# A hybrid attention block on one core: order of the last operand splits and division of the final normalisation

## The chip, the cores and the metric

The kernel runs on one core of one Trainium2 chip. The metric is the device time of one execution in microseconds (us), the median over the runs of a comparison. A profile of one execution is read beside it: every instruction of TensorE (PE), VectorE (DVE), ScalarE (ACT), GpSimd (POOL) and of the DMA queues, with start and duration.

## The reference

One encoder layer on 1024 tokens of width 1024. The input is projected once; the columns are queries, keys, values and gates of two groups of heads. Group A attends over a neighbourhood on a 16 x 64 grid, group B over a window of 128 tokens with a sink. Each output is multiplied by SiLU of its gate, then projected, added to the scaled input and normalised:

```python
h = jnp.einsum('bsd,de->bse', x, w_in[layer])
...
mixed = jnp.concatenate([y_a * jax.nn.silu(z_a), y_b * jax.nn.silu(z_b)], axis=-1)
y = jnp.einsum('bse,ed->bsd', mixed, w_out[layer])
x = layer_norm(DEEPNORM_ALPHA * x + y, ln_gain[layer], ln_bias[layer])
```

layer_norm takes mean and variance over the 1024 columns of a token, and ends with gain and bias.

## The kernel before, in words

**Arithmetic.** Products on PE are made of halves: a float32 operand is split into a float16 high part, `h`, and a low part, `l`, which is the float32 value less `h`. A product is three matmuls, high by high, high by low and low by high. For a split ACT casts the high part and DVE or POOL subtracts.

**Stages.** Input projection, attention over 128 units with the rest of the projection filled in between the units (`pump_to`, L1076), and the output projection with the normalisation (`final`, L1325). Each engine runs its instructions in the order in which the program gives them; ahead of `final` that order comes from a planner with costs and due times (`Op`, `enq`, `pop`), in `final` it is written out by hand (L1440 to L1540).

**Output projection.** It is a seven-product scheme on halves of tokens and of columns. The mixed activations lie transposed in eight z tiles, 128 inner columns by 1024 tokens, taken as four pairs (za, zb) (`ZP`, L43). `ZL` is tokens 0 to 511, `ZH` 512 to 1023. Of each pair come A11 (za, ZL), A12 (zb, ZL), A22 (zb, ZH), S3 = za ZL - za ZH, S2 = zb ZH - S3, S1 = za ZH + zb ZH and S4 = zb ZL - S2; S3, S2, S1 and S4 are made in place, in za ZL, za ZL, za ZH and zb ZL. The weights give B11, B21, B22 and T1 to T4. The products (`TERMS`, L1293) are q1 = A11 B11, q2 = A12 B21, q3 = S4 B22, p4 = A22 T4, q5 = S1 T1, q6 = S2 T2 and q7 = S3 T3, each summed over the four pairs. A product for one tile of 128 tokens is 12 matmuls of 512 columns. `prod` (L1298) issues them; its matmuls are all L1308.

**Banks.** Products share PSUM banks: b[t] takes q1, then q6, then q7, then p4; cb[t] takes q5, then q3; a[t] takes q2. Between two of them `add` (L1341) reads the bank on DVE and adds it, scaled, to the 512 columns of an output row tile in SBUF (`xr`, which holds alpha times the input): `add(t, a, ...)` for row tile t and column half a. So the next product in a bank waits for that addition. q1 of all tiles, and all but the last pair of q2 for tiles 0 and 1, are under way when `final` begins.

**Last pair.** z tiles 2 and 3 are done last. `m_last` (L1542) makes what is still to be made of them, with `za` for tile 2 and `z` for tile 3. `hi` is a cast on ACT (L1549), `lo` a subtraction on DVE or POOL (L1552). `first` scales row tile 0 by alpha on ACT; `between` is the first addition, `add(0, 0, b[0])`, which reads q1. Ahead of it in `final` DVE fills `eps` and `nident`, the negative identity (L1328 to L1331). PE then goes on with q5 for the first three pairs, q2's last pair for tiles 0 and 1 (L1493, L1494), q6(0), q5's last pair, q7(0), q3(0), q6(1) and so on. Loads of the row tiles 5, 2, 6, 3 and 7 (`x_load`, L1334) stand on SP's queue, in that order, with gain and bias between.

**Normalisation.** As a half row gets its last addition (`whole=True`), `bn` takes statistics of it in chunks. `row_stats` and `row_scale` give mean and reciprocal deviation. `norm` (L1415) splits the work of a row tile between DVE (columns 512 to 1023, with gain and bias copied into PSUM as gp and bp) and ACT with POOL (columns 0 to 511; tiles 0, 4 and 7 all columns). Row tile 7 and then row tile 3 are last. For tile 7 ACT normalises two halves (L1423), and POOL multiplies by the gain and adds the bias (`norm_half`, L1432). For tile 3 the last 512 columns of the product come in three parts of 256, 128 and 128: `norm_last` (L1377) does columns 512 to 1023 and 384 to 511 on DVE with PSUM copies of gain and bias (gp, bp, gq), and columns 0 to 383 on PE, as a sum of three products with the identity: row times gain (the gain multiplied in ahead by POOL, `norm_ahead`, L1374), minus mean times gain, plus deviation times bias; ACT scales it out. Matmuls on a zero tile `warm` keep PE running before that (L1380). Four output transfers end the kernel: tile 3 in three parts (L1401, L1403, and L1404 on ACT's queue) and tile 7's second half (L1438).

Of the kernel before, what the change touches and what calls it, by code (L numbers as in the profile page):

```python
# [7 lines left out]
F32 = mybir.dt.float32  # L8
# [4 lines left out]
AF = mybir.ActivationFunctionType  # L13
# [9 lines left out]
EPS = 1e-5  # L23
# [47 lines left out]
def hybrid_block(ctx, tc, xT, x, wt, wv, wo, bias, sink, gain, lbias, cos, sin, bmask, out):  # L71
    nc = tc.nc
# [37 lines left out]

    identf = const.tile([128, 128], F32, name="identf")
    make_identity(nc, identf)
    vb = zp.tile([128, 8, 2, 2, HD], F16, tag="zv", name="vb", bufs=1)
    vsc = const.tile([128, 1], F32, name="vsc")
    vrs = const.tile([128, 1], F32, name="vrs")
# [23 lines left out]
    nc.vector.memset(warm, 0.0)  # L139
    ones = const.tile([128, 128], BF16, name="ones")  # L140
    nc.vector.memset(ones, 2.0 ** -13)
    bm = const.tile([128, 320], F32, name="bm")
    sk = const.tile([128, 4], F32, name="sk")
    nsk = const.tile([128, 4], F32, name="nsk")
# [1180 lines left out]
    def final():  # L1325
        actx.close()
        fp = ctx.enter_context(tc.tile_pool(name="fp", bufs=2, reuse_waits="tile"))
        eps = fp.tile([128, 1], F32, name="eps", bufs=1)  # L1328
        nc.vector.memset(eps, EPS)
        nident = fp.tile([128, 128], F32, name="nident", bufs=1)  # L1330
        nc.vector.tensor_scalar_mul(nident, identf, -1.0)  # L1331
        xrs, stats = xr_, {}

        def x_load(t):  # L1334
# [14 lines left out]
        def bn(t, a, c):  # L1349
            o, w = c  # L1350
            if t not in stats:
                stats[t] = fp.tile([128, 8, 6], F32, name=f"stats{t}", bufs=1)
            b = 128 if t == 3 else 512
            for i in range(w // b):
                n = (512 * a + o) // b + i
                nc.vector.bn_stats(stats[t][:, n, :], xrs[t][:, b * n:b * n + b])

        def row_stats(t):
            mv = fp.tile([128, 2], F32, tag="mv", name="mv")
            nc.vector.bn_aggr(mv, stats[t][:, :8 if t == 3 else 2, :])  # L1360
            sd = fp.tile([128, 1], F32, tag="sd", name="sd")
            nc.scalar.activation(sd, mv[:, 1:2], AF.Sqrt, bias=eps)
            return mv, sd
# [5 lines left out]
            nc.vector.tensor_scalar(nmr, mv[:, 0:1], rstd, -1.0, op0=ALU.mult, op1=ALU.mult)  # L1369
            return rstd, nmr  # L1370

        HP, HQ, H1 = slice(0, 384), slice(384, 512), slice(512, 1024)

        def norm_ahead(t):  # L1374
            nc.gpsimd.tensor_mul(xrs[t][:, HP], xrs[t][:, HP], gb[:, HP])
# [1 line left out]
        def norm_last(t):  # L1377
            ts = slice(128 * t, 128 * t + 128)
            xr, pn = xrs[t], bank("t")
            for _ in range(28):  # L1380
                nc.tensor.matmul(gq[:, :128], warm, warm, start=True, stop=True)
            nc.tensor.matmul(pn[:, HP], identf, xr[:, HP], start=True, stop=False)
            dm, ds = (fp.tile([128, 128], F32, name=n, bufs=1) for n in ("dm", "ds"))
            mv = fp.tile([128, 2], F32, tag="mv", name="mv")
            nc.vector.bn_aggr(mv, stats[t])
            sd = fp.tile([128, 1], F32, tag="sd", name="sd")
            nc.scalar.activation(dm, nident, AF.Copy, scale=mv[:, 0:1])
            nc.scalar.activation(sd, mv[:, 1:2], AF.Sqrt, bias=eps)
            nc.scalar.activation(ds, identf, AF.Copy, scale=sd)
            rstd = fp.tile([128, 1], F32, tag="rstd", name="rstd")  # L1390
            nc.tensor.matmul(pn[:, HP], dm, gb[:, HP], start=False, stop=False)
            nc.tensor.matmul(pn[:, HP], ds, bb[:, HP], start=False, stop=True)
            halves = (H1, gp, bp), (HQ, gq[:, 128:256], gq[:, 256:384])
            for h, g, _ in halves:
                nc.vector.scalar_tensor_tensor(xr[:, h], xr[:, h], mv[:, 0:1], g, op0=ALU.subtract, op1=ALU.mult)
                if h is H1:
                    nc.vector.reciprocal(rstd, sd)
            for h, _, o in halves:
                nc.vector.scalar_tensor_tensor(xr[:, h], xr[:, h], rstd, o, op0=ALU.mult, op1=ALU.add)
                if h is H1:  # L1400
                    nc.sync.dma_start(out[ts, h], xr[:, h])  # L1401
            nc.scalar.activation(xr[:, HP], pn[:, HP], AF.Copy, scale=rstd)
            nc.sync.dma_start(out[ts, HQ], xr[:, HQ])  # L1403
            nc.scalar.dma_start(out[ts, HP], xr[:, HP])  # L1404
# [10 lines left out]
        def norm(t, *st_):  # L1415
            ts = slice(128 * t, 128 * t + 128)
            xr, ha, hb = xrs[t], slice(512, 1024), slice(0, 512)
            mv, sd = st_ or row_stats(t)
            rstd, nmr = row_scale(mv, sd)
            both = t in (0, 4, 7)  # L1420
            h = slice(0, 1024) if both else hb
            for h in (hb, ha) if t == 7 else (h,):
                nc.scalar.activation(xr[:, h], xr[:, h], AF.Identity, bias=nmr, scale=rstd)  # L1423
            if not both:
                nc.vector.scalar_tensor_tensor(xr[:, ha], xr[:, ha], mv[:, 0:1], gp, op0=ALU.subtract, op1=ALU.mult)
                nc.vector.scalar_tensor_tensor(xr[:, ha], xr[:, ha], rstd, bp, op0=ALU.mult, op1=ALU.add)
                nc.sync.dma_start(out[ts, ha], xr[:, ha])
            for h in (ha, hb) if both else (hb,):
                if t != 7:
                    norm_half(t, h)  # L1430

        def norm_half(t, h, between=None):  # L1432
            xr = xrs[t]
            nc.gpsimd.tensor_mul(xr[:, h], xr[:, h], gb[:, h])  # L1434
            if between:
                between()
            nc.gpsimd.tensor_add(xr[:, h], xr[:, h], bb[:, h])
            nc.sync.dma_start(out[128 * t:128 * t + 128, h], xr[:, h])  # L1438
# [82 lines left out]
        q7(2)  # L1521
        c11(2)
        gq = bank("s")
        nc.scalar.copy(gq[:, 128:256], gb[:, HQ])
        nc.scalar.copy(gq[:, 256:384], bb[:, HQ])
        q3(2)
        q6(3)
        p4(2)
# [13 lines left out]
    def m_last(first, between):  # L1542
        z, za = zt[ZP[3][1]], zt[ZP[3][0]]
        need(*done["S3", 3])
        for key in ("A12", "A22", "S1", "S2", "S4"):
            m_home(key, 3)

        def hi(key, src):
            nc.scalar.copy(part[key, 3][0], src)  # L1549

        def lo(eng, key, src):
            eng.tensor_sub(part[key, 3][1], src, part[key, 3][0])  # L1552

        hi("A12", z[:, ZL])
        first()
        nc.vector.tensor_sub(za[:, ZL], z[:, ZH], za[:, ZL])  # L1556
        nc.gpsimd.tensor_add(za[:, ZH], za[:, ZH], z[:, ZH])
        lo(nc.vector, "A12", z[:, ZL])
        hi("S2", za[:, ZL])
        hi("A22", z[:, ZH])  # L1560
        nc.vector.tensor_sub(z[:, ZL], z[:, ZL], za[:, ZL])
        between()
        lo(nc.vector, "S2", za[:, ZL])
        lo(nc.gpsimd, "A22", z[:, ZH])
        hi("S4", z[:, ZL])
        lo(nc.vector, "S4", z[:, ZL])
        hi("S1", za[:, ZH])
        lo(nc.gpsimd, "S1", za[:, ZH])

    fill.extend((out_head((0,), range(3), "pj"), out_head((1,), range(3), "pj"), out_head((0, 1), (3,), None),  # L1570
                 out_head((0,), range(3), "s", "q2"), out_head((1,), range(3), "s", "q2"),
# [190 lines left out]
```

## Time and profile before

| what | us |
|---|---|
| runs | 435.64, 436.56, 436.87 |
| median | 436.56 |
| the profiled execution | 434.77 |
| its span | 432.9 |
| PE busy | 425.5 |
| DVE busy | 347.6 |
| ACT busy | 315.9 |
| POOL busy | 291.2 |

In lines of the timeline the first number is the start in us from the span's start, the second the time to the end of the group; then engine, line of the kernel, operation, and output <- inputs by tile name with shapes; x is the count of instructions merged. Square brackets hold the idle time of the engine before the group, and what ended it. In lines of a group the numbers are durations in ns (least, median, greatest) and the first and last start. In lines of a window come its bounds and length, the busy time and count of PE, weight loads, DVE, ACT and POOL, then PE's granted clock, the busy share of the 16 DMA engines and GB/s.

### The profile page before, as it was taken

To read this page: it belongs to the slowest core of one execution; us is meant where nothing else is said; L and a number is where in the kernel's file an instruction comes from. 1 tells how busy PE (TensorE), PEld (TensorE's weight loads), DVE (VectorE), ACT (ScalarE), POOL (GpSimd) and SP (SyncE) were. 2 spreads that over 40 slices of the span, in tenths; PEclk is the share of its full clock that TensorE was granted. 3 is DMA by queue.
4 is the path that set the end of the run, shared out by engine and by line. 5 is a ranking of instruction groups with operands and counts; after the bars stand their busy time and mean duration, and the time that the engine had idled before them with its cause. 6 is when DMAs were issued, how large, how long until landed. Compare 5 with 4: busy or idle time off the path is not lost.

```text
span 432.9 us, 9414 instructions
## 1 busy us (share of the span) xinstructions
PE 425.5 (98%) x3197; PEld 249.3 (58%) x3197; DVE 347.6 (80%) x861; ACT 315.9 (73%) x677; POOL 291.2 (67%) x298
## 2 busy tenths in 40 slices
PE   9999999999999999999999999999999999899995
PEld 8997754444455656565556555565655655344444
DVE  5978976884987879888788997878888876787685
ACT  5849779787669989788988868889788883643222
POOL 0110085778568767879999976767889799458245
PEclk9999999999999999999999999999999999999999
DMA  7947759982349999989879999997999899923122
GB/s 267 406 145 256 238 177 324 286 269 89 118 140 190 205 157 209 210 186 151 171 167 221 199 196 176 249 182 141 221 186 214 149 143 281 414 111 123 73 98 99
DMA packets 131409, 84.82 MB, mean 196 GB/s; under 512 B 97568, under 2 KB 106656, under 8 KB 131360
## 3 DMA queue, kind: packets, MB, share of 16 engines
q1 hardware_dynamic: 131216, 84.02, 79.8%
q8 instruction: 25, 0.41, 0.4%
q14 instruction: 24, 0.20, 0.2%
q10 hardware_dynamic: 144, 0.20, 0.1%
HBM read 50.60 MB, written 10.52 MB: 141 GB/s over the span
## 4 chain that ended last, share of the span: by engine, by line
PE 95%; DVE 2%; POOL 1%; issue 0%; POOLq 0%; ACT 0%; ACTq 0%
PE ps_pj L457 50%; PE ps_t L996 7%; PE ps_s L1308 6%; PE ps_s L564 6%; PE ps_pj L1308 5%; PE ps_s L919 4%; PE ps_s L920 4%; PE ps_t L1308 3%; PE ps_pj L564 3%; PE ps_t L564 3%; PE ps_t L1033 2%; PE ps_t L490 1%; POOL xr L1434 1%; DVE A L1552 0%; DVE z L1556 0%
## 5 line engine op out<-in xcount | busy, mean ns | idle before, releaser
L457 PE MATMUL ps_pj<-xf,wh 128*128 128x512 f16 x672 | 201.3, 379 | 0.0
L457 PE MATMUL ps_pj<-xf,wl 128*128 128x512 f16 x336 | 127.3, 379 | 0.0
L457 PEld LDWEIGHTS <-wh 128*128 128x128 f16 x672 | 63.8, 98 | 58.3
L949 ACT ACTIVATE ps_s<-sn,nm 128x321 f32<-128x321 f32 (+3 forms) x128 | 67.7, 529 | 33.5 <-DVE nm L933 32.3
L968 DVE SCALAR_TENSOR_TENSOR split<-ps_s,split 128x320 f16<-128x320 f32 (+2 forms) x128 | 62.6, 489 | 17.9 <-ACT split L967 16.2
L253 POOL TENSOR_SCALAR wr<-wr,wsc 128x512 f32<-128x512 f32 x32 | 24.0, 749 | 56.3 <-ACT wh L248 48.5
L967 ACT ACTIVATE split<-ps_s 128x320 f16<-128x320 f32 (+2 forms) x128 | 55.1, 430 | 2.0 <-DMA tr<-split 0.4
L457 PEld LDWEIGHTS <-wl 128*128 128x128 f16 x336 | 32.9, 98 | 37.8
L933 DVE CUSTOM_DVE_ANT_0 sn<-ps_s,bm,nsk 128x320 f32<-128x320 f32 (+2 forms) x64 | 36.9, 577 | 9.9 <-PE ps_s L920 9.7
L254 POOL TENSOR_TENSOR wl<-wr,wh 128x512 f16<-128x512 f32 x32 | 39.6, 1238 | 2.7
L933 DVE CUSTOM_DVE_ANT_0 sn<-ps_s,bias,sg 128x368 f32<-128x368 f32 (+1 forms) x64 | 36.1, 564 | 4.4 <-PE ps_s L920 4.0
L920 PE MATMUL ps_s<-ks,qs 128*128 128x320 f16 (+3 forms) x128 | 38.2, 298 | 0.0
L919 PE MATMUL ps_s<-ks,qs 128*128 128x320 f16 (+3 forms) x128 | 38.2, 298 | 0.0
L996 PEld LDWEIGHTS <-tr 128*128 128x128 f16 (+1 forms) x1056 | 36.2, 98 | 1.8
L367 POOL COPY ks<-ks 64x512 f16<-64x512 f16 x40 | 25.9, 649 | 8.1 <-ACT ks L311 5.7
L1308 PEld LDWEIGHTS <-m 128*128 128x128 f16 x186 | 17.7, 98 | 20.6 <-issue 1.5
L1434 POOL TENSOR_TENSOR xr<-xr,gb 128x512 f32<-128x512 f32 x10 | 12.7, 1273 | 21.1 <-ACT xr L1423 21.1
L248 ACT ACTIVATE wh<-wr,wsc 128x512 f16<-128x512 f32 x32 | 22.7, 710 | 0.9 <-DVE wsc L278 0.9
L564 PEld LDWEIGHTS <-xf 128*128 128x128 f16 x192 | 18.6, 98 | 7.2
L919 PEld LDWEIGHTS <-qs 128*128 128x128 f16 x128 | 12.5, 98 | 15.1
L920 PEld LDWEIGHTS <-qs 128*128 128x128 f16 x128 | 12.5, 98 | 15.0
L996 PE MATMUL ps_t<-va,tr 128*128 128x65 f16 (+1 forms) x528 | 19.1, 193 | 0.0
(265 smaller groups left out, 934.8 us busy)
## 6 DMA issues: line engine op xcount, KB each, us to landing
wr<-in_wt SPq DMA_DIRECT2D x32, 256.0 KB, 3.2
ws<-in_wt SPq DMA_DIRECT2D x15, 512.0 KB, 5.6
wor<-in_wo SPq DMA_DIRECT2D x20, 256.0 KB, 3.9
xr<-in_x SPq DMA_DIRECT2D x8, 512.0 KB, 9.5
out<-xr SPq DMA_DIRECT2D x15, 256.0 KB, 2.0
bias<-in_bias SPq DMA_DIRECT2D x8, 440.0 KB, 4.7
wob<-in_wo SPq DMA_DIRECT2D x12, 256.0 KB, 3.9
wvraw<-in_wv SPq DMA_DIRECT2D x9, 320.0 KB, 5.6
```

What stands on the lines that cost most here:

```text
L254: nc.gpsimd.tensor_sub(l, raw, h)
L367: nc.gpsimd.tensor_copy(place(t, o, half, col), place(t, a, half, col))
L457: nc.tensor.matmul(ps, a[:, k % 4, :], mv, start=(k == 0 and i == 0), stop=(k == KT - 1 and i == 2))
L564: nc.tensor.matmul(ps[:, :320], lh[:, ts], rh[:, cs], start=(k == ko[0] and i == 0), stop=(k == ko[-1] and i == 2))
L919: nc.tensor.matmul(ps[:, :n], q, sl[0], start=True, stop=False)
L920: nc.tensor.matmul(ps[:, :n], q, sl[1], start=False, stop=True)
L933: nc.vector.tensor_tensor_reduce(sn[:, at0:at0 + n], ps[:, :n], bias_t, sg[:, c:c + 1], init, op0=ALU.add, op1=ALU.min, accum_out=nm)
L949: nc.scalar.activation(pt[:, c], sn[:, c], AF.Exp, bias=nm, scale=-1.0, accum_out=acc)
L967: nc.scalar.activation(h, pt[:, c], AF.Copy, scale=PSCALE)
L968: nc.vector.scalar_tensor_tensor(l, pt[:, c], PSCALE, h, op0=ALU.mult, op1=ALU.subtract)
L996: nc.tensor.matmul(ps[:, w * m:w * m + e], a, b_, start=(i == 0), stop=(i == len(mms) - 1))
L1308: nc.tensor.matmul(ps[:, cs], lh[:, 128 * t:128 * t + 128], rh[:, cs], start=(fresh and e == 0 and n == 0), stop=(e == len(terms) - 1 and ...
```

## The change

In the last pair (`m_last`):

- A12's low part comes first on DVE, then the first addition, then S2's subtraction; before, S2's subtraction stood ahead of A12's low part, and S4's subtraction ahead of the addition.
- S1 comes ahead of A22 on ACT and POOL and ahead of S4; before, it was last.
- `eps` is filled among the kernel's constants, and `nident` is made by ACT later, beside the copies of gain and bias for the last tile.

At the end:

- PE and ACT normalise columns 0 to 255 of row tile 3 for 0 to 383, DVE 256 to 511 for 384 to 511; gq holds gain and bias for 256 columns each, and the warm-up matmuls write to the bank a[3] for gq.
- The warm-up matmuls are 10 and 16, with the identity product between, for 28 ahead of it.
- Statistics of row tile 3 are taken in one chunk per addition: 512, 256, 128 and 128 columns, for eight chunks of 128.
- The first half of row tile 7 is normalised on ACT, and multiplied by the gain on POOL, in two parts of 256 columns.

```diff
+    eps = const.tile([128, 1], F32, name="eps")
...
+    nc.vector.memset(eps, EPS)
...
-        eps = fp.tile([128, 1], F32, name="eps", bufs=1)
-        nc.vector.memset(eps, EPS)
         nident = fp.tile([128, 128], F32, name="nident", bufs=1)
-        nc.vector.tensor_scalar_mul(nident, identf, -1.0)
...
         def bn(t, a, c):
             o, w = c
             if t not in stats:
-                stats[t] = fp.tile([128, 8, 6], F32, name=f"stats{t}", bufs=1)
-            b = 128 if t == 3 else 512
-            for i in range(w // b):
-                n = (512 * a + o) // b + i
-                nc.vector.bn_stats(stats[t][:, n, :], xrs[t][:, b * n:b * n + b])
+                stats[t] = fp.tile([128, 4, 6], F32, name=f"stats{t}", bufs=1), []
+            tile_, seen = stats[t]
+            seen.append(c)
+            nc.vector.bn_stats(tile_[:, len(seen) - 1, :], xrs[t][:, 512 * a + o:512 * a + o + w])
+
+        def aggregate(t, mv):
+            tile_, seen = stats[t]
+            nc.vector.bn_aggr(mv, tile_[:, :len(seen), :])
...
-        HP, HQ, H1 = slice(0, 384), slice(384, 512), slice(512, 1024)
+        HP, HQ, H1 = slice(0, 256), slice(256, 512), slice(512, 1024)
...
-            for _ in range(28):
-                nc.tensor.matmul(gq[:, :128], warm, warm, start=True, stop=True)
+
+            def spin(n):
+                for _ in range(n):
+                    nc.tensor.matmul(a[3][:, :128], warm, warm, start=True, stop=True)
+
+            spin(10)
             nc.tensor.matmul(pn[:, HP], identf, xr[:, HP], start=True, stop=False)
+            spin(16)
...
-            halves = (H1, gp, bp), (HQ, gq[:, 128:256], gq[:, 256:384])
+            halves = (H1, gp, bp), (HQ, gq[:, :256], gq[:, 256:])
...
-            for h in (hb, ha) if t == 7 else (h,):
+            for h in (*quarters, ha) if t == 7 else (h,):
                 nc.scalar.activation(xr[:, h], xr[:, h], AF.Identity, bias=nmr, scale=rstd)
...
+        quarters = slice(0, 256), slice(256, 512)
+
         def norm_half(t, h, between=None):
             xr = xrs[t]
-            nc.gpsimd.tensor_mul(xr[:, h], xr[:, h], gb[:, h])
+            for c in quarters if between else (h,):
+                nc.gpsimd.tensor_mul(xr[:, c], xr[:, c], gb[:, c])
...
-        nc.scalar.copy(gq[:, 128:256], gb[:, HQ])
-        nc.scalar.copy(gq[:, 256:384], bb[:, HQ])
+        nc.scalar.copy(gq[:, :256], gb[:, HQ])
+        nc.scalar.copy(gq[:, 256:], bb[:, HQ])
+        nc.scalar.activation(nident, identf, AF.Copy, scale=-1.0)
...
         hi("A12", z[:, ZL])
         first()
+        lo(nc.vector, "A12", z[:, ZL])
+        between()
+        nc.gpsimd.tensor_add(za[:, ZH], za[:, ZH], z[:, ZH])
         nc.vector.tensor_sub(za[:, ZL], z[:, ZH], za[:, ZL])
-        nc.gpsimd.tensor_add(za[:, ZH], za[:, ZH], z[:, ZH])
-        lo(nc.vector, "A12", z[:, ZL])
         hi("S2", za[:, ZL])
+        hi("S1", za[:, ZH])
         hi("A22", z[:, ZH])
+        lo(nc.vector, "S2", za[:, ZL])
+        lo(nc.gpsimd, "S1", za[:, ZH])
         nc.vector.tensor_sub(z[:, ZL], z[:, ZL], za[:, ZL])
-        between()
-        lo(nc.vector, "S2", za[:, ZL])
         lo(nc.gpsimd, "A22", z[:, ZH])
         hi("S4", z[:, ZL])
         lo(nc.vector, "S4", z[:, ZL])
-        hi("S1", za[:, ZH])
-        lo(nc.gpsimd, "S1", za[:, ZH])
```

More of the change, by code (lines that the diff above doesn't have):

```diff
@@ L1351, in bn @@
             if t not in stats:
-                stats[t] = fp.tile([128, 8, 6], F32, name=f"stats{t}", bufs=1)
-            b = 128 if t == 3 else 512
-            for i in range(w // b):
-                n = (512 * a + o) // b + i
-                nc.vector.bn_stats(stats[t][:, n, :], xrs[t][:, b * n:b * n + b])
+                stats[t] = fp.tile([128, 4, 6], F32, name=f"stats{t}", bufs=1), []
[5 more added lines that the diff above has]
+            nc.vector.bn_aggr(mv, tile_[:, :len(seen), :])
         def row_stats(t):
             mv = fp.tile([128, 2], F32, tag="mv", name="mv")
-            nc.vector.bn_aggr(mv, stats[t][:, :8 if t == 3 else 2, :])
+            aggregate(t, mv)
             sd = fp.tile([128, 1], F32, tag="sd", name="sd")
@@ L1379, in norm_last @@
             xr, pn = xrs[t], bank("t")
-            for _ in range(28):
-                nc.tensor.matmul(gq[:, :128], warm, warm, start=True, stop=True)
+            def spin(n):
+                for _ in range(n):
+                    nc.tensor.matmul(a[3][:, :128], warm, warm, start=True, stop=True)
+            spin(10)
             nc.tensor.matmul(pn[:, HP], identf, xr[:, HP], start=True, stop=False)
+            spin(16)
             dm, ds = (fp.tile([128, 128], F32, name=n, bufs=1) for n in ("dm", "ds"))
             mv = fp.tile([128, 2], F32, tag="mv", name="mv")
-            nc.vector.bn_aggr(mv, stats[t])
+            aggregate(t, mv)
             sd = fp.tile([128, 1], F32, tag="sd", name="sd")
```

## The prediction

> **What bounds the kernel.** I read the page first, then the chain of waits, then the timeline engine by engine over the last pair of z tiles and over the end.
>
> ```profile
> span 432.9 us, 9414 instructions
> PE 95%; DVE 2%; POOL 1%; issue 0%; POOLq 0%; ACT 0%; ACTq 0%
> ```
>
> The profiled run took 434.77 us: 432.9 of span and 1.9 around it. The median of the three runs is 436.56, so it lies 1.8 below it; I work out a difference on the trace and take it from the median. PE carries 95% of the chain, so only holes in PE's stream and the tail behind its last matmul are worth anything. Both lie where the change works.
>
> ```profile
> 368.01 0.59 PE L1308 MATMUL ps_s<-wo,A 128*128 128x512 f16 x2
> 369.49 1.04 PE L1308 MATMUL ps_s<-wo,A 128*128 128x512 f16 x4 [0.89 <-DVE A L1552]
> 371.71 0.59 PE L1308 MATMUL ps_pj<-T,m 128*128 128x512 f16 x2 [1.18 <-DVE xr L1344]
> 375.59 0.38 PE L1308 MATMUL ps_pj<-T,m 128*128 128x512 f16 x1
> 380.77 0.59 PE L1308 MATMUL ps_pj<-T,m 128*128 128x512 f16 x2
> ```
>
> These are PE's two holes: the end of q2 waits for A12's low part, q6(0) for the first addition, which must read the bank before q6(0) goes on in it. From 371.71 (q6(0)) to 375.59 (q7(0)) lie 18 matmuls, 0.216 us each. q2's six from 368.01 would be through at 369.30; q6(0) starts at 371.71, so the two holes together cost 2.41 us. The 0.89 and 1.18 sum to less because the matmul in flight is counted as busy. Why DVE is late:
>
> ```profile
> 364.32 0.75 DVE L1039 SCALAR_TENSOR_TENSOR z<-ps_t,zc,z 128x512 f32<-128x512 f32 x1 [2.39 <-PE ps_t L1033]
> 365.00 1.17 DVE L1331 TENSOR_SCALAR nident<-identf 128x128 f32<-128x128 f32 x1
> 365.02 0.06 DVE L1329 MEMSET eps<- 128x1 f32 x1
> 366.10 1.66 DVE L1556 TENSOR_TENSOR z<-z,z 128x512 f32<-128x512 f32 x1
> 367.68 1.76 DVE L1552 TENSOR_TENSOR A<-z,A 128x512 f16<-128x512 f32 x1
> 369.47 1.53 DVE L1561 TENSOR_TENSOR z<-z,z 128x512 f32<-128x512 f32 x1
> 370.92 0.74 DVE L1344 SCALAR_TENSOR_TENSOR xr<-ps_pj,yc,xr 128x512 f32<-128x512 f32 x1
> 371.58 0.68 DVE L1552 TENSOR_TENSOR S<-z,S 128x512 f16<-128x512 f32 x1
> ```
>
> ```profile
> 364.93 1.16 POOL L1102 TENSOR_TENSOR tp<-tl,tp 128x512 f16<-128x512 f32 x1
> 366.04 1.17 POOL L1229 TENSOR_TENSOR z<-z 128x512 f16<-128x512 f32 x1
> 367.16 1.73 POOL L1557 TENSOR_TENSOR z<-z,z 128x512 f32<-128x512 f32 x1
> 369.00 1.44 POOL L1552 TENSOR_TENSOR A<-z,A 128x512 f16<-128x512 f32 x1
> ```
>
> DVE and POOL take turns. L1556 stands at 366.10, POOL's L1229 ends at 367.21, L1556 ends at 367.76: 0.55 after it. POOL's L1557, started at 367.16, ends 1.13 after that, at 368.89; DVE's L1552 ends at 369.44, again 0.55 later; POOL's next one at 370.44, 1.00 later; L1561 at 371.00. An operation of two SBUF operands that takes 0.68 alone (371.58) thus takes 1.5 to 1.8 here, and A12's low part stands third in the queue, the addition fifth.
>
> **The change in the last pair.** eps and nident leave DVE. eps becomes a 0.06 us memset among the constants, before any data is in: nothing. nident goes to ACT, beside the copies of gain and bias, which double: less than one cast of 512 columns (0.62, below) for nident and about another half for the copies, at a time when ACT only waits for the next tile's statistics and PE has products queued. If that cover were gone it would be 1 us on ACT; I take nothing.
>
> ```profile
> 365.11 0.62 ACT L1549 CAST A<-z 128x512 f16<-128x512 f32 x1 [0.72 <-DVE z L1039]
> 365.64 1.06 ACT L1339 ACTIVATE xr<-xr 128x1024 f32<-128x1024 f32 x1
> 367.79 0.62 ACT L1549 CAST S<-z 128x512 f16<-128x512 f32 x1 [1.09 <-DVE z L1556]
> ```
>
> New order, with the 0.55 and 1.0 to 1.13 above. A12's high part ends at 365.73; its low part asks for its turn at 365.76 and gets it when POOL's L1102 ends, 366.09: done 366.64. PE wants it as the third of q2's matmuls, at 368.44: hole one is gone with 1.8 to spare. POOL's L1229 then runs to 367.65. The addition reads PSUM (0.74, no turn needed) and waits for row tile 0's scaling, 366.70: done 367.47, 1.8 ahead of q6(0) at 369.30: hole two is gone. S2's subtraction takes its turn at 367.65, done 368.20; POOL's sum for S1 369.33; ACT casts S2 by 368.86, S1 by 370.0, A22 by 370.5. S2's low part waits for POOL's sum, done 369.88; q6(0) wants it with its last matmul, 369.30 + 11 x 0.216 = 371.68. S4's subtraction 370.43; S1's low part on POOL, blocked till then, 371.44; q5 wants it with its third matmul, 371.90 + 0.43 = 372.33. S4's low part follows at 371.99, A22's at 373.0; their products come later. Next on DVE is the addition that reads q6(0): its last matmul ends at 372.06, so it runs to 372.86, and q7(0), which writes that bank, comes at 369.30 + 18 x 0.216 = 373.19. That margin, 0.33, is the smallest of the stage. Moved along with S1 is no DMA; SP's queue keeps its order. What ACT queues behind S1's cast, A22's and S4's casts, waits for POOL's sum with it; this is in the times above.
>
> The Trainium skill speaks against one spot of this. Its page "SBUF — State Buffer", section "Who interferes with whom", says that a DVE instruction with two SBUF inputs and a GpSimd one that reads SBUF block each other fully and that issue order decides. S1's low part, now on POOL between DVE's two steps for S4, asks at about 370.1, S4's subtraction at 369.8; by that rule DVE goes first by 0.3, and the gain stays 2.4, but with the order turned S4 and the addition behind it come 1.0 later. The trace agrees on the order where L1556 (366.10) goes ahead of L1557 (367.16).
>
> **Behind it.** x tile 5 may become the pace:
>
> ```profile
> 365.64 3.97 SPq L1336 DMA_DIRECT2D xr<-in_x  x3
> 375.71 1.06 ACT L1339 ACTIVATE xr<-xr 128x1024 f32<-128x1024 f32 x1 [1.59 <-issue]
> 376.80 0.75 DVE L1344 SCALAR_TENSOR_TENSOR xr<-ps_t,yc,xr 128x512 f32<-128x512 f32 x1 [0.84 <-ACT xr L1339]
> 377.47 0.74 DVE L1344 SCALAR_TENSOR_TENSOR xr<-ps_pj,yc,xr 128x512 f32<-128x512 f32 x1
> ```
>
> Its load is the first of the three that SP issues from 365.64; no engine ends ACT's 1.59 of idle time, so it is that transfer. Nothing in the change moves it: ACT's scaling stays at 375.71 and the two additions end at 378.21. q6(1) writes the bank of the second, and starts at 380.77 - 2.41 = 378.36. It just fits: 0.15. So PE's stream moves ahead by 2.4, and by no more than about 2.55.
>
> **The change at the end.**
>
> ```profile
> 422.41 1.52 ACT L1423 ACTIVATE xr<-xr,nmr,rstd 128x512 f32<-128x512 f32 x2 [0.48 <-DVE nmr L1369]
> 423.20 0.87 DVE L1356 BATCH_NORM_STATS2 stats<-xr 128x6 f32<-128x128 f32 x4
> 423.99 0.47 DVE L1344 SCALAR_TENSOR_TENSOR xr<-ps_t,yc,xr 128x256 f32<-128x256 f32 x1
> 424.49 0.49 DVE L1356 BATCH_NORM_STATS2 stats<-xr 128x6 f32<-128x128 f32 x2
> 424.89 0.33 DVE L1344 SCALAR_TENSOR_TENSOR xr<-ps_s,yc,xr 128x128 f32<-128x128 f32 x1
> L1356 DVE BATCH_NORM_STATS2 stats<-xr x22: 275/694/695, 378.9 to 425.8; 128x6 f32<-128x512 f32 x14, 128x6 f32<-128x128 f32 x8
> L1360 DVE BATCH_NORM_AGGREGATE mv<-stats x7: 208/209/210, 383.8 to 421.3; 128x2 f32<-128x12 f32 x7
> 426.17 0.37 DVE L1385 BATCH_NORM_AGGREGATE mv<-stats 128x2 f32<-128x48 f32 x1
> 424.58 0.96 POOL xr L1375
> 428.33 0.33 SPq L1401 DMA_DIRECT2D out<-xr  x1
> 429.29 0.39 ACTq L1404 DMA_DIRECT2D out<-xr  x1
> 429.37 0.33 SPq L1438 DMA_DIRECT2D out<-xr  x1
> 429.20:430.10 0.90, 0.00 (x0) 0.00 (x0) 0.00 (x0) 0.06 (x1) 0.14 (x1) 1.00 0.98 337
> 430.30:431.30 1.00, 0.00 (x0) 0.00 (x0) 0.00 (x0) 0.00 (x0) 0.00 (x0) 0.81 1.02 379
> ```
>
> Statistics: four chunks of 128 (0.87) become one of 512 (0.69): 0.18. Two of 128 (0.49) become one of 256, by the line through 0.275 and 0.694 about 0.42: 0.07. The aggregate reads 24 values, between 0.21 for 12 and 0.37 for 48: 0.26, so 0.11. The mean comes 0.36 earlier. Against it DVE's two passes over the last columns are 256 wide for 128, 0.47 for 0.33: one stands ahead of the first output's DMA (428.33), which moves by 0.36 - 0.14 = 0.22, both ahead of the second. ACT and PE handle 256 columns for 384: ACT's DMA, 429.29, comes about 0.8 earlier. POOL's multiply ahead shrinks from 0.96 to some 0.67 (256/384 of it is 0.64, plus a little that does not shrink): 0.29. Its chain starts from a quarter: ACT's halves take 0.76 each, so at best 0.38 sooner; I take 0.2, and 0.1 off for the instruction more. Its last DMA, 429.37, comes about 0.4 earlier. The warm-up matmuls, two fewer and split by the identity product, are not on this path.
>
> But four output transfers, 768 KB, follow the 428.33 issue, and the DMA engines are full from 429.2 to 431.4 (shares 0.98 and 1.02). So the end moves with the first of the four, 0.22, plus the short gap between the two full stretches, 0.2, of which I take half: 0.3, from 0.2 (bandwidth alone) to 0.4 (latency alone).
>
> Sum: 2.41 + 0.3 = 2.7 us. 434.77 becomes 432.07; the median 436.56 becomes 433.9. Uncertain by 0.5 below (PE gains 2.2, the tail 0.2 or less) and 0.2 above, so 433.5 to 434.4. 0.3% of the median, about what a measurement of this kernel can tell, is 1.31 us.
>
> **Rivals.** *The turns fall the other way.* At 366.09 POOL's queued L1229 could go first. Then A12's low part ends at 367.76 (still in time), the addition at 368.4, S2's subtraction at 369.44, its low part 370.8, and S4's low part, behind one or both of POOL's low parts, at 372.9 to 373.9. The addition for q6(0) ends 0.67 after that, 373.6 to 374.6, and q7(0) waits 0.4 to 1.4. Gain 1.3 to 2.3 with the tail: 434.3 to 435.3. For it: margins of 0.33 rest on some ten steps. Against it: nident, asking at 365.0 while L1102 ran, ended at 366.17, ahead of L1229.
>
> *DVE's queue behind x tile 5.* Each 1 us that the tile lands later than the margin of 0.15 costs PE 1 us, as additions run in order. Half a microsecond to 1.5 later: gain 1.3 to 2.3, 434.3 to 435.2. The transfers do not depend on the change; they may vary.
>
> *It does not do what it says.* The holes move instead of closing, to q7(0) and q6(1) together, and the tail is all: gain 0.3 to 1, 435.6 to 436.3.
>
> *Slower.* The pool of the final stage loses eps at its head and half of each statistics tile, so its x buffers lie over other tiles of the attention stage. If x tile 5's buffer then waits for a later reader, its issue slips; it decides from 2.7 + 0.15 = 2.85 us on. Were it to go out only where the third of those loads goes now, 3.6 us later, PE would lose 3.5, and the run would take 436.56 + 3.5 - 2.7 = 437.4. For it: PE has nothing else to do at q6(1). Against it: the attention stage's last reader, the transposes ahead of L1039 (364.32), is through before the load goes out.
>
> **Chances.** Forecast 0.60; turns 0.17, two thirds of it over 1.31; x tile 5 0.13, again two thirds; no effect 0.06; slower 0.04. Faster 0.60 + 0.11 + 0.09 = 0.80, same 0.06 + 0.04 + 0.06 = 0.16, slower 0.04. Range: down to 433.0, as the runs spread 0.9 below their median; up to 436.0, the two middle rivals' ends and some of the third.
>
> **What would show it.** Right: no idle time of PE between q2 and q6(0); A12's low part done near 366.6 and the addition near 367.5; q7(0) without a wait; q6(1) at most 0.2 after the addition from x tile 5's queue; the aggregate 0.36 sooner against the last matmul; the DMA full until the end. Wrong: POOL's L1229 ahead of A12's low part; a wait before q7(0) or q6(1); a table load on ACT for nident; the last transfer bound by POOL and not by the first output.

## The result, and the profile after

| | before | after |
|---|---|---|
| median, same comparison (22 runs each) | 435.73 | 433.17 |
| range of the runs | 433.91 to 438.08 | 432.34 to 435.76 |
| the profiled execution | 434.77 | 433.83 |
| its span | 432.9 | 431.8 |

The ratio is 0.995, with a 95% interval from 0.9934 to 0.9966: 2.2 us less, between 1.5 and 2.9. The forecast, 2.7 less, lies inside. The absolute time came out at 433.17 for 433.9 forecast, mostly because the kernel before has a lower median in this comparison (435.73) than in its first three runs (436.56).

The page of the kernel after opens like the one of before, and DVE's share of the chain has fallen from 2% to 1%:

```profile
span 431.8 us, 9407 instructions
PE 96%; DMA 1%; POOL 1%; DVE 1%; POOLq 0%; ACT 0%; issue 0%; ACTq 0%
```

The spans differ by only 1.1 us, less than half of the forecast. Before that is taken for a weaker effect, look at where the last pair begins. PE's timeline of after, first matmuls of the last transposes, q2, q6(0), q7(0) and q6(1):

```profile
365.33 0.60 PE L1035 MATMUL ps_t<-identf,on 128*128 128x128 f32 x4
...
369.66 1.46 PE L1310 MATMUL ps_s<-wo,A 128*128 128x512 f16 x6
370.95 1.46 PE L1310 MATMUL ps_pj<-T,m 128*128 128x512 f16 x6
374.84 1.46 PE L1310 MATMUL ps_pj<-T,m 128*128 128x512 f16 x6
380.02 1.46 PE L1310 MATMUL ps_pj<-T,m 128*128 128x512 f16 x6
```

q2 starts at 369.66, where it started at 368.01 before: after enters the stage 1.65 us late, though nothing that runs up to the last transposes differs except eps' memset of 0.06 us. From there on it is faster. q2 runs through in 1.29 (369.66 to 370.95; before 3.70, to 371.71), so both holes are gone: 2.41 became 0. q6(1) has no wait either.

DVE's timeline of after over the same stage shows why:

```profile
365.97 0.75 DVE L1041 SCALAR_TENSOR_TENSOR z<-ps_t,zc,z 128x512 f32<-128x512 f32 x1 [2.38 <-PE ps_t L1035]
367.41 0.86 DVE L1563 TENSOR_TENSOR A<-z,A 128x512 f16<-128x512 f32 x1 [0.68 <-ACT A L1560]
368.37 0.75 DVE L1343 SCALAR_TENSOR_TENSOR xr<-ps_pj,yc,xr 128x512 f32<-128x512 f32 x1
369.04 0.80 DVE L1570 TENSOR_TENSOR z<-z,z 128x512 f32<-128x512 f32 x1
370.52 0.99 DVE L1563 TENSOR_TENSOR S<-z,S 128x512 f16<-128x512 f32 x1 [0.68 <-ACT S L1560]
371.44 0.68 DVE L1576 TENSOR_TENSOR z<-z,z 128x512 f32<-128x512 f32 x1
372.80 0.88 DVE L1563 TENSOR_TENSOR m<-z,m 128x512 f16<-128x512 f32 x1 [0.69 <-ACT m L1560]
373.74 0.75 DVE L1343 SCALAR_TENSOR_TENSOR xr<-ps_pj,yc,xr 128x512 f32<-128x512 f32 x1
...
379.16 0.74 DVE L1343 SCALAR_TENSOR_TENSOR xr<-ps_pj,yc,xr 128x512 f32<-128x512 f32 x1
```

A12's low part (the line that writes A) ends at 368.27 and the first addition at 369.12, both before q2 itself has begun. The addition that reads q6(0) ends at 374.49, 0.35 ahead of q7(0); the last of x tile 5's at 379.90, 0.12 ahead of q6(1).

At the end, the outputs' DMA issues on SP's queue and then the one on ACT's, after:

```profile
427.36 0.33 SPq L1408 DMA_DIRECT2D out<-xr  x1
...
428.28 0.38 SPq L1448 DMA_DIRECT2D out<-xr  x1
```

```profile
427.84 0.37 ACTq L1411 DMA_DIRECT2D out<-xr  x1
```

Counted from the first matmul of q3(3)'s 256 columns (422.21 before, 421.46 after), the first issue moved from 6.12 to 5.90, ACT's from 7.08 to 6.38, the last one of SP from 7.16 to 6.82, and the end of the span from 10.71 to 10.39 (the page gives spans to 0.1; the packed trace has 432.918 and 431.848).

### The profile page after: what moved, and what is told of

The parts are those of the page before. It is cut to its first block, busy times and chain, and to the rows that moved or that the text cites. A ratio compares the mean times of both kernels' runs of the same rounds, so it can differ in the third digit from the quotient of the medians.

```text
span 431.8 us, 9407 instructions
## 1 busy us (share of the span) xinstructions
PE 425.8 (99%) x3195; PEld 250.5 (58%) x3195; DVE 343.2 (79%) x856; ACT 317.1 (73%) x679; POOL 291.3 (67%) x299
## 4 chain that ended last, share of the span: by engine, by line
PE 96%; DMA 1%; POOL 1%; DVE 1%; POOLq 0%; ACT 0%; issue 0%; ACTq 0%
PE ps_pj L459 50%; PE ps_t L998 7%; PE ps_s L1310 7%; PE ps_s L566 6%; PE ps_pj L1310 5%; PE ps_t L1310 4%; PE ps_s L921 4%; PE ps_s L922 4%; PE ps_pj L566 3%; PE ps_t L566 3%; PE ps_t L1035 2%; DMA tr<-split 1%; PE ps_t L492 1%; POOL xr L1444 1%; POOLq L1769 0%; POOL xr L1447 0%
## 5 line engine op out<-in xcount | busy, mean ns | idle before, releaser
L1444 POOL TENSOR_TENSOR xr<-xr,gb 128x512 f32<-128x512 f32 (+1 forms) x11 | 12.9, 1175 | 18.5 <-ACT xr L1430 18.5
L566 PE MATMUL ps_s<-wvh,x 128*128 128x320 f32 x64 | 19.1, 319 | 0.0
```

The costliest lines, as they stand in the source:

```text
L566: nc.tensor.matmul(ps[:, :320], lh[:, ts], rh[:, cs], start=(k == ko[0] and i == 0), stop=(k == ko[-1] and i == 2))
```

## The two profiles differ upstream

Of the 1.65 us, 1.04 arise in the first microseconds. PE's timeline of before and then of after, two of the first 128x320 matmuls, the same instructions in both kernels:

```profile
4.45 0.31 PE L564 MATMUL ps_pj<-wvh,x 128*128 128x320 f32 x1
4.59 0.30 PE L564 MATMUL ps_s<-wvh,x 128*128 128x320 f32 x1
```

```profile
4.53 0.47 PE L566 MATMUL ps_pj<-wvh,x 128*128 128x320 f32 x1
4.80 0.47 PE L566 MATMUL ps_s<-wvh,x 128*128 128x320 f32 x1
```

They start about 0.15 apart in one execution and 0.267 in the other. The remaining 0.6 stands in a transposing transfer that came later, the one DMA piece in the chain of after:

```profile
161.12 5.14 DMA tr<-split
```

Neither is an effect of the change: q2's start varies from 368.01 to 369.74 over the profiles of this study, all of them with the same work up to there. The experiments are therefore read from two stretches that do not contain it. **The stage** runs from the first of the last transposes to q6(1): 17.08 before, 14.69 after (365.33 to 380.02), 2.39 less. **The end** runs from q3(3)'s 256 columns to the end of the span: 10.71 and 10.39, 0.32 less. (The expectations below were written with 10.69 and 10.34, from the page's rounded spans.) Between them, from q6(1) to those columns, lie 41.44 us in every profile.

Profiles of the same code repeat well in the new kernel's two stretches: the stage is 14.68 or 14.69 in after and in experiments 7 to 11, and the end 10.39 to 10.41 in after and in experiments 4 to 6. The old end is 10.70 and 10.71 in experiments 1 and 2. The old stage varies more (experiment 3).

The DMA view gives the busy share of the DMA engines in tenths. Asked for the 1 us from 8.5 behind the columns, in slices of 0.025 us, it shows when the last packets begin: before, then after.

```profile
DMA  5997995997995994898499499669422000000000
```

```profile
DMA  9496992968999297240000000000000000000000
```

The last busy slice ends at 9.28 before and at 8.95 after, so the transfers end 0.33 earlier, as much as the kernel does.

## The experiments

The theory: the gain is the two holes (2.4, needing the new order and DVE without nident) plus some 0.3 at the end. The rivals: one part does all of it; or margins, not the order, decide.

**1. The new order alone** (before, with eps and nident still on DVE).

```diff
         hi("A12", z[:, ZL])
         first()
+        lo(nc.vector, "A12", z[:, ZL])
+        between()
+        nc.gpsimd.tensor_add(za[:, ZH], za[:, ZH], z[:, ZH])
         nc.vector.tensor_sub(za[:, ZL], z[:, ZH], za[:, ZL])
-        nc.gpsimd.tensor_add(za[:, ZH], za[:, ZH], z[:, ZH])
-        lo(nc.vector, "A12", z[:, ZL])
...
```

> The kernel before with the new order of the last pair alone; eps and nident stay on DVE ahead of it, the end is the old one. Stage = from the last transposes ahead of the last z tile (L1033) to the start of q6(1): 17.08 us before, 14.69 after. Theory (DVE and POOL take turns, so both the order and the two instructions ahead of it count): nident takes the first turn at 366.1, POOL's low part the next, so every step on DVE comes 1.1 us later than after; A12's low part (367.8 on the clock of before) and the first addition (368.4) are still in time, but S4's low part ends near 373.9 or 372.9 and the addition that reads q6(0) makes q7(0) wait 1.45 or 0.45. Stage 15.1 to 16.1, gain against before 1.0 to 2.0, likelier 1.0. Rival (the order alone is the whole gain, the two small instructions are hidden): stage 14.7, gain 2.4, no wait ahead of q7(0).

434.72 us, ratio 0.9984 (0.9965 to 1.0002). The stage takes 16.03, a gain of 1.05 (one profile, like the stages and ends below). PE's timeline, q7(0):

```profile
375.76 1.46 PE L1308 MATMUL ps_pj<-T,m 128*128 128x512 f16 x6 [1.19 <-DVE xr L1344]
```

DVE's timeline of the same kernel, and then POOL's queued instruction:

```profile
366.22 1.05 DVE L1331 TENSOR_SCALAR nident<-identf 128x128 f32<-128x128 f32 x1
366.25 0.06 DVE L1329 MEMSET eps<- 128x1 f32 x1
367.19 1.67 DVE L1552 TENSOR_TENSOR A<-z,A 128x512 f16<-128x512 f32 x1
...
371.82 1.66 DVE L1565 TENSOR_TENSOR z<-z,z 128x512 f32<-128x512 f32 x1
```

```profile
367.14 1.16 POOL L1229 TENSOR_TENSOR z<-z 128x512 f16<-128x512 f32 x1
```

Both old holes are gone, but q7(0) now waits: it starts 5.24 behind q6(0) (370.52), where after has 3.89, so 1.35 are lost. nident holds DVE while POOL's product runs, POOL's queued instruction goes next, and A12's low part takes 1.67 for 0.86. One turn lost at the head is not recovered: four steps later S4's subtraction takes 1.66 for 0.68. This is the mechanism of the rival "The turns fall the other way", brought about by nident; in the full change it did not come.

**2. eps and nident away from DVE alone** (before, with the old order).

```diff
-        nc.vector.tensor_scalar_mul(nident, identf, -1.0)
...
+        nc.scalar.activation(nident, identf, AF.Copy, scale=-1.0)
```

> The kernel before with eps among the constants and nident on ACT, nothing else; order of the last pair and end as before. Theory (turns): S2's subtraction takes the turn at 366.1 that nident had; all of DVE comes 1.1 us earlier. A12's low part ends near 368.2, in time, hole one is gone; the first addition ends near 370.5, q6(0) waits 1.3 for it instead of the 2.4 of both holes. Stage (L1033 to q6(1)) 17.08 - 1.1 = 16.0, gain 1.1. With e1 at 1.0 the two do not add to 2.4: each alone leaves a wait of another kind. Rival (eps and nident cost DVE nothing that PE sees, 0.06 and 0.1 us of work): gain 0.1 or less.

434.48 us, ratio 0.9979 (0.9963 to 0.9994); the stage takes 15.96, a gain of 1.1. PE's timeline, q6(0):

```profile
372.31 1.46 PE L1310 MATMUL ps_pj<-T,m 128*128 128x512 f16 x6 [1.11 <-DVE xr L1343]
```

The first hole is closed, the second not, since the addition still stands behind S4's subtraction. So each of the two edits is worth about 1.1 alone, and together they give 2.4: neither is the whole.

**3. The edits at the end alone** (before, with the 256 columns, the fewer chunks, the split warm-up and tile 7's parts).

```diff
-        HP, HQ, H1 = slice(0, 384), slice(384, 512), slice(512, 1024)
+        HP, HQ, H1 = slice(0, 256), slice(256, 512), slice(512, 1024)
...
```

> The kernel before with the edits at the end alone: 256 columns on PE, fewer chunks, tile 7 in quarters, warm-up split; the last pair with eps and nident as before. End = from the first matmul of q3(3)'s 256 columns to the end of the span: 10.69 us before, 10.34 after. Theory (the DMA engines are full behind the first of four outputs, so the end moves with it): end 10.35, stage of the last pair 17.08 as before, time 0.35 us or 0.08% less, too little for a verdict. Rival (part of the gain of 2.2 to 2.7 us comes from the end): 1 us or more.

435.41 us, ratio 1.0001 (0.9983 to 1.0019). The times cannot show 0.3 us; the profile does: the end takes 10.47, 0.24 less than before. Its last packets begin at 8.95, exactly as in after. The 0.08 that it ends later stand behind them: the trace's last instruction is a semaphore event of DVE, 0.09 behind those of all other engines. Experiments 10 and 11 show the same, no other profile does, and the cause stays open. The stage took 16.83 for 17.08 with the same instructions: nident waited 0.91 there and not 1.17, as POOL's product had begun earlier against DVE. That much the holes vary by themselves.

**4. Is x tile 5 the next wait?** (after, with its load second, not first).

```diff
-        x_load(5)
...
+        x_load(5)
```

> The kernel after, with the load of x tile 5 behind that of x tile 2 on SP's queue; everything else the same. Theory (x tile 5 has a margin of 0.12 to 0.15 us, and past it DVE's queue, in order, holds back q6(1) one for one): as second of the loads it lands 1.2 to 2.0 us later, q6(1) waits 1.1 to 1.9, the stage L1033 to q6(1) is 15.8 to 16.6 against 14.69, the time 1.1 to 1.9 more than after. Rival (the transfer is hidden; PE has other work or the additions catch up): no change against after.

434.70 us, ratio to before 0.9982 (0.9962 to 1.0001); the stage takes 16.31, 1.62 more than in after. PE's timeline, q6(1), and then ACT's, the tile's scaling:

```profile
381.34 1.02 PE L1310 MATMUL ps_pj<-T,m 128*128 128x512 f16 x4 [1.47 <-DVE xr L1343]
```

```profile
378.79 1.06 ACT L1338 ACTIVATE xr<-xr 128x1024 f32<-128x1024 f32 x1 [4.41 <-DMA xr<-in_x]
```

The scaling waits for the load, the additions for the scaling, and PE for them. The rival "DVE's queue behind x tile 5" is a real mechanism and takes over when the load slips; in after it keeps clear by 0.12 us.

**5. The addition back behind S4's subtraction** (after, one call moved).

```diff
-        between()
...
         nc.vector.tensor_sub(z[:, ZL], z[:, ZL], za[:, ZL])
+        between()
```

> The kernel after, with the first addition back behind S4's subtraction, as it stood before; A12's low part stays first. Theory (q6(0) writes the bank that the addition reads, and the addition waits its turn in DVE's queue): hole one stays closed, the addition ends 1.85 us after q6(0) could start; a wait of 1.9 ahead of q6(0), stage L1033 to q6(1) 16.6 against 14.69 after and 17.08 before. Rival (A12's low part was the whole wait and the addition only followed it): no wait, stage 14.7.

434.83 us, ratio to before 0.9984 (0.9967 to 1.0002); the stage takes 16.56, 1.87 more. PE's timeline, q6(0):

```profile
372.79 1.46 PE L1310 MATMUL ps_pj<-T,m 128*128 128x512 f16 x6 [1.72 <-DVE xr L1343]
```

**6. S1 last again** (after, S1's cast and low part behind S4's).

```diff
-        hi("S1", za[:, ZH])
-        lo(nc.gpsimd, "S1", za[:, ZH])
...
         lo(nc.vector, "S4", z[:, ZL])
+        hi("S1", za[:, ZH])
+        lo(nc.gpsimd, "S1", za[:, ZH])
```

> The kernel after, with S1's cast and low part last, behind S4's, as before. Theory: with q6(0) 2.4 us earlier S1 no longer comes in time; its cast ends 0.7 us after q5 wants it and its low part on POOL about 1.5 after: waits of 1.5 in all ahead of and within q5, stage 16.2. Rival (S1's place does not matter, POOL is not late): stage 14.7.

434.69 us, ratio to before 0.9982 (0.9969 to 0.9995); the stage takes 16.33, 1.64 more. PE's timeline, two places in q5:

```profile
373.52 0.61 PE L1310 MATMUL ps_t<-tp,S 128*128 128x512 f16 x2 [0.67 <-ACT S L1560]
...
374.76 1.04 PE L1310 MATMUL ps_t<-tp,S 128*128 128x512 f16 x4 [0.64 <-POOL S L1563]
```

With the holes closed, q5 arrives 2.4 us sooner and asks for S1 sooner. Part of the price is a lost turn again: A22's low part now stands ahead of S1's on POOL and starts at 370.24, S4's subtraction at 370.60 takes 1.64 for 0.68, and S4's cast and S1's behind it come that much later. What moving S1 up earns by itself was not run; without it most of the gain at the holes is given back here.

**7. Statistics back to eight chunks** (after, with 256 columns kept).

```diff
...
-            seen.append(c)
-            nc.vector.bn_stats(tile_[:, len(seen) - 1, :], xrs[t][:, 512 * a + o:512 * a + o + w])
+            b = 128 if t == 3 else 512
+            for i in range(w // b):
+                seen.append(c)
+                p = 512 * a + o + b * i
+                nc.vector.bn_stats(tile_[:, len(seen) - 1, :], xrs[t][:, p:p + b])
```

> The kernel after, with the statistics of row tile 3 in eight chunks of 128 columns again; else as after. Theory (DVE's chain to the first output sets the end): mean and first output 0.36 us later, end 10.34 + 0.3 = 10.65. Rival (POOL's chain sets the end): end 10.34.

433.13 us, a single time. The end takes 10.74, 0.35 more than in after; the last packets begin at 9.30, also 0.35 later; the first output's issue comes 6.25 after the columns' start (420.61), 0.35 later than in after:

```profile
426.86 0.33 SPq L1411 DMA_DIRECT2D out<-xr  x1
```

**8. 384 columns on PE and ACT again** (after, with the fewer chunks kept).

```diff
-        HP, HQ, H1 = slice(0, 256), slice(256, 512), slice(512, 1024)
+        HP, HQ, H1 = slice(0, 384), slice(384, 512), slice(512, 1024)
...
```

> The kernel after, with 384 columns of row tile 3 on PE and ACT and 128 on DVE again; fewer chunks, quarters and split warm-up stay. Theory (DMA engines full behind the first output): DVE's first output goes out 0.14 us earlier, ACT's 0.6 to 0.8 later and as the last of the four; the same 768 KB, so the end (q3(3)'s first matmul to the end of the span; 10.34 after) moves between -0.1 and +0.2. Rival (the size of PE's share is what shortened the end): +0.3 or more.

433.69 us, a single time; the end takes 10.69, 0.30 more than in after and 0.02 less than before. My theory, that this share is off the path, falls. The first issue is even earlier than in after, 5.77 against 5.90. What is later is ACT's DMA, 7.16 after the columns' start (421.10) for 6.38. ACT's timeline and queue:

```profile
427.65 0.58 ACT L1409 ACTIVATE xr<-ps_t,rstd 128x384 f32<-128x384 f32 x1 [1.51 <-PE ps_t L1399]
...
428.26 0.37 ACTq L1411 DMA_DIRECT2D out<-xr  x1
```

The DMA view shows what that does, from 425 to 432 us in 40 slices of 0.175 us; here of this kernel, then of after:

```profile
DMA  0000000069992005999880099998991000000000
```

```profile
DMA  0000000029997000006999999999995000000000
```

In after the engines stay full from 428.15 until the last byte, so the first issue sets the end. With 384 columns they run dry from 428.7 to 429.0, two slices below one tenth: what was issued first is through, and the last two transfers have not begun. There the last issues set the end; the last packets begin at 9.23, 0.28 later than in after.

**9. Tile 7's first half in one piece** (after, without the quarters).

```diff
-            for h in (*quarters, ha) if t == 7 else (h,):
+            for h in (hb, ha) if t == 7 else (h,):
...
-            for c in quarters if between else (h,):
+            for c in (h,):
```

> The kernel after, with row tile 7's first half in one piece on ACT and POOL again. Theory: POOL's chain starts 0.2 us later and has one instruction less, its last output is issued 0.1 later, inside the stretch in which the DMA engines are full: end 10.34 to 10.4. Rival (POOL's chain sets the end): 10.45 or more.

433.38 us, a single time; the end takes 10.40, 0.01 more than in after, within what the same code repeats: the quarters show no gain.

**10. Row tile 3's last 512 columns out in two parts** (after, each sent before DVE's passes over 256 to 511).

```diff
...
+            for c in (0, 256):
+                h = slice(512 + c, 768 + c)
+                shifted(h, bp[:, c:c + 256])
+                nc.sync.dma_start(out[ts, h], xr[:, h])
+            scaled(HQ, gq[:, :256])
+            shifted(HQ, gq[:, 256:])
```

> The kernel after, with the first output of row tile 3 (columns 512 to 1023) finished and sent in two parts of 256 columns, ahead of both passes over columns 256 to 511. Theory (the DMA engines are full from the first of the last outputs on, so the end moves with its issue until POOL's last output binds): first issue 0.5 us earlier, end (q3(3)'s first matmul to the end of the span) 10.34 - 0.3 = 10.05. Rival (the end is set by POOL's chain and the fixed time of its last transfer): end 10.3 to 10.5, as that last issue moves by 0 to 0.2 later.

433.35 us, ratio to before 0.9946 (0.9929 to 0.9962); the end takes 10.40, no gain on after's 10.39. SP's queue:

```profile
426.91 0.81 SPq L1411 DMA_DIRECT2D out<-xr  x2
428.21 0.33 SPq L1415 DMA_DIRECT2D out<-xr  x1
428.64 0.40 SPq L1453 DMA_DIRECT2D out<-xr  x1
```

The first issue is 0.52 earlier against the columns (5.38 from 421.53), as meant, and the last one 0.29 later (7.11), queued on SP behind the second pass over HQ. The transfers do end sooner: their last packets begin at 8.80 for 8.95. The end does not follow, as 1.6 us pass behind them for 1.4 in after; 0.09 of that is DVE's late semaphore event.

**11. Six transfers on two queues** (10, with HQ's DMA on ACT's queue and tile 7's second half in two parts as well).

```diff
-            nc.sync.dma_start(out[ts, HQ], xr[:, HQ])
+            nc.scalar.dma_start(out[ts, HQ], xr[:, HQ])
...
+            for c in parts or (h,):
+                nc.gpsimd.tensor_add(xr[:, c], xr[:, c], bb[:, c])
+                nc.sync.dma_start(out[128 * t:128 * t + 128, c], xr[:, c])
```

> The kernel after, with row tile 3's columns 512 to 1023 and row tile 7's second half each finished and sent in two parts of 256 columns, and row tile 3's columns 256 to 511 sent on ACT's queue behind ACT's own. In the run with row tile 3's two parts alone the first issue came 0.45 us earlier but the last one 0.28 later, behind another transfer on SP, and the end stayed. Theory (the end is the later of two bounds, 3.5 us from the first issue and 2.1 from the last large one): both move, end 10.34 - 0.3 to 0.45 = 9.9 to 10.05; time 0.3 us less than after, too little to tell from it in the median. Rival (six transfers cost what they spare, or POOL's chain binds): end 10.3 or more.

433.39 us, ratio to before 0.9956 (0.9937 to 0.9976); the end takes 10.51, 0.12 more than in after, where I expected less. SP's queue and the DMA view, in the slices of experiment 8:

```profile
425.77 0.81 SPq L1411 DMA_DIRECT2D out<-xr  x2
426.67 1.00 SPq L1454 DMA_DIRECT2D out<-xr  x2
```

```profile
DMA  0039994007958949999999970000000000000100
```

The first issue is at 5.39 and the last at 6.96. But the same 768 KB take 15 slices (2.6 us, from 426.6 to 429.2) where after needs 13 (2.2), and the row dips to 5 and to 4 tenths on the way. At after's rate a part of 128 KB takes 0.37 us, an estimate, and SP issues the first three 0.42 and 0.48 apart (425.77, 426.19, 426.67). So the engines would run dry in between, which fits the dips but is not shown to be all of it. The last packets still begin 0.10 sooner than in after, at 8.85; the rest is lost behind them. No version that was tried has a shorter end than after.

## Why the prediction was right, and where it was not

**The holes.** The 2.41 came out whole (3.70 from q2 to q6(0) became 1.29), and the stage as 2.39. Subtracting the 1.65 of the later start, A12's low part ends at 366.62 (forecast 366.64), the first addition at 367.47 (367.47), S2's low part at 369.86 (369.88), S4's subtraction at 370.47 (370.43), S4's low part at 372.03 (371.99), the addition that reads q6(0) at 372.84 (372.86). The two numbers from which this was worked out, DVE 0.55 after POOL's end and POOL 1.0 to 1.13 after DVE's, carry to another order of the same operations. POOL's timeline of after shows them at the head:

```profile
366.57 1.16 POOL L1104 TENSOR_TENSOR tp<-tl,tp 128x512 f16<-128x512 f32 x1
367.69 1.60 POOL L1231 TENSOR_TENSOR z<-z 128x512 f16<-128x512 f32 x1
...
371.70 1.44 POOL L1563 TENSOR_TENSOR S<-z,S 128x512 f16<-128x512 f32 x1 [0.73 <-ACT S L1560]
```

POOL's first one ends at 367.73; A12's low part, waiting since 367.41, ends 0.54 later, ahead of POOL's L1231, which then ends 1.02 after that.

**The spot that the rule on ports spoke of.** The Trainium skill, page "SBUF — State Buffer", section "Who interferes with whom", lets issue order decide between S4's subtraction and S1's low part. In after DVE's subtraction starts at 371.44 and POOL's low part at 371.70. DVE goes first, by 0.26 where 0.3 was forecast, and takes 0.68, its time alone. Here trace and rule agree.

**nident on ACT and S1's place** were costed at nothing, and each cover held: ACT's additional work shows in no wait of PE, and experiment 6 gives the price of the old place, 1.64, a lost turn of S4's subtraction included.

**The margins** were 0.35 and 0.12 for 0.33 and 0.15. The second agrees in part by luck: over the six profiles with this last pair the addition ends 0.12 to 0.84 ahead of q6(1), as x tile 5 lands at different times. Experiments 1 and 4 bring the two middle rivals about, at or just above the prices given: 1.35 for the turns (forecast 0.4 to 1.4), 1.62 for x tile 5 (0.5 to 1.5). So the chances put on them were for mechanisms that exist. The rival "Slower" did not come: q6(1) starts without a wait, so x tile 5 was in time; where its buffer lies was not looked into.

**The end** was forecast at 0.3 and measured at 0.32. Its steps held: the mean 0.35 earlier (forecast 0.36), the first issue 0.22 (0.22), ACT's 0.70 (0.8), SP's last 0.34 (0.4). **What failed is the step from them to the end**: "So the end moves with the first of the four". The sum did add half of the gap between the two full stretches, 0.1, but named no edit that closes it, and it left out ACT's and PE's smaller share, which does. Experiments 7 and 8 each undo one half, and each loses the whole: 0.35 and 0.30. Before stood at both bounds together. Take 0.8 us from an issue to its first bytes (427.36 to 428.15 in after) and 2.2 us for the four transfers' 768 KB. For before the first issue then gives 428.33 + 0.8 + 2.2 = 431.3. Its last two transfers, 192 and 256 KB at the same rate, 1.3 us, give 429.29 + 0.8 + 1.3 = 431.4. The DMA view of before, in the slices of experiment 8, shows the last two begin just as the first two are through (5 tenths in the slice from 430.08):

```profile
DMA  0000000000000009998000029999959999997000
```

With two bounds 0.1 apart, moving one earns nothing; the change moved both, by 0.22 and 0.7. In experiment 8 the same sum gives 429.9 by the first issue and 428.19 + 0.8 + 1.3 = 430.3 by the last two, and the gap in its DMA row shows that the second holds. For after both sums give 427.36 + 0.8 + 2.2 = 430.4 at most. Counted from the columns, the sum ends before's transfers at 9.2 and after's at 8.9, where the last packets begin at 9.28 and 8.95: 0.3, all of the gain. The total was right because both edits were made at once, not because the first alone decides.

This sum holds to 0.1 for the kernels with four transfers. For experiments 10 and 11, with five and six, it ends the transfers 0.25 and 0.34 earlier than after's; their last packets begin 0.15 and 0.10 earlier, and the kernels end 0.01 and 0.12 later. So the smaller transfers spare less than the sum says, and what they spare is lost behind the last packets, where 1.6 and 1.7 us pass for 1.4 in before and in after. Why stays open.

**The absolute time.** 433.17 lies 0.7 below the forecast. The lower median of before in this comparison gives 0.8 of that; the medians differ by 2.56, 0.1 less than forecast. The profiles' two stretches say 2.39 + 0.32 = 2.71, and the interval of the ratio, 1.5 to 2.9 us, holds both. The forecast's "433.5 to 434.4" should begin at 433.7 by its own 0.2; 433.17 lies below it for the reason just given.

## What to carry to other kernels

When two engines take turns, work the order out turn by turn with the measured ends, from the operation that holds the turn at the head of the queue: one lost turn there came back as a 1.35 us wait of PE. When a wait is closed, ask which operands the work behind it now wants sooner, and move their makers up in the same edit: S1's old place alone would have taken back 1.64 of the 2.4. Where several transfers end a kernel, sum from each issue what it and all later ones carry, and take the latest end (it held for four transfers here, not for five or six smaller ones): an edit that serves only one of two nearly equal bounds shows no gain.

## What the runs showed of the hardware that was not expected

The same matmuls of 320 columns started about 0.15 us apart in one profiled execution and 0.267 in the other, while the granted clock was 1.00 in both. Here are the windows from 4 to 6 us, before and then after:

```profile
4.00:6.00 2.00, 2.00 (x12) 1.87 (x13) 1.76 (x5) 0.48 (x2) 0.00 (x0) 1.00 0.90 289
```

```profile
4.00:6.00 2.00, 2.00 (x8) 2.00 (x9) 1.70 (x5) 0.85 (x2) 0.00 (x0) 1.00 0.99 307
```

PE got 12 matmuls under way in one and 8 in the other, and the difference stayed to the end as 1.04 us. The Trainium skill, page "TensorE: Matmul & The Clock Gate", section "Part 1: The HAM clock gate (the "warmup" mystery)", says that the array runs at half clock until a free-running window has seen it busy, at 1.2 GHz for one column a cycle, and that this point varies from run to run. By that page 320 columns would take 0.267 us at half clock, an estimate that agrees with the 0.267 measured. The granted clock in the windows does not show it, so that this is the cause remains argued. Whatever it is, it moves the spans of two single profiles by as much as some of the edits here, and only stretches that begin behind it can be compared.
